# Delta-rule recurrence: the products of the inverses with the right-hand side in four quarters of the array, batch 1's chunks exchanged over the partitions

## The chip, the core and the metric

The kernel runs on one core of a Trainium2 chip. TensorE (PE in the profile, its weight loads PEld) multiplies, VectorE (DVE), ScalarE (ACT) and GpSimd (POOL) do the elementwise work, and POOL and SyncE (SP) issue most of the transfers. The metric is the device time of one execution in microseconds (us).

## What is computed

One encoder layer on two batches of 256 tokens, float32. The part that the change touches is the gated delta rule of 8 heads, run in both directions over 4 chunks of 64 tokens. Per head and direction the reference does this, where `u` and `w` are products of the inverse `t_mat` of a 64 by 64 triangular matrix:

```python
def step(S, inp):
    q_i, k_i, u_i, w_i, g_i, qk_i = inp
    v_new = u_i - einsum('bhcd,bhde->bhce', w_i, S)
    o = einsum('bhcd,bhde->bhce', q_i * exp(g_i), S) + einsum('bhcs,bhse->bhce', qk_i, v_new)
    S = S * exp(g_last) + einsum('bhcd,bhce->bhde', k_i * exp(g_last - g_i), v_new)
    return S, o
```

## The kernel before

Nearly all of the time is matrix products: `half_gemm` multiplies 8 weight blocks of 128 by 128, each split into a high and a low part, with 512 token columns; these are the rows `ps_g`. The recurrence is threaded between them. `recur` is a generator, one for each head, and two heads (h and h+1) run side by side (`recur_pair`, `together`): what one head issues up to its next `yield` is followed directly by what the other issues. `half_gemm` calls `pump` after every second weight block, and each call lets the generators go on by one `yield`; `pause(n)` skips n calls. TensorE's instructions keep exactly the order in which they are written (`pin`), so TensorE stands still when one of them has to wait. ACT's and DVE's order is set by a scheduler; `load_w` asks it to put the split of a weight block (`w_hi` on ACT, `w_lo` on DVE) ahead of other work.

Each head has 4 steps (`st`). A partition half (`half[hf]`) carries one chunk of one direction, and a step treats both halves of both batches b. In a step:

- `pks` (from step 1 on): four products of the keys and queries with the state S.
- `rv`: the right-hand side, four DVE operations, from `pks`. In step 0 it is a slice of `dvn`, so the products of step 0 are named `dvn,uq` in the profile and those of steps 1 to 3 `r,uq`.
- `os`: four ACT operations (DVE in step 2) that also read `pks`.
- `pn`: the product of the inverse in `uq[st]` with `rv`, 128 by 128 per batch. Half of the 128 by 128 matrix is zero: it holds a 64 by 64 block in two opposite corners, and `open_recurrence` clears the tiles once for that.
- `n`: an ACT copy of `pn` out of PSUM, both batches in one operation of 128 by 256 elements.
- after `pause(N_GAP)`: the new state from `n` and `kd` (rows `n,kd`), and the output part from `n` and `uq` (rows `ps_o<-n,uq`), four products each.

PSUM tiles for all of these come from the pool `psm`, which has three buffers (`sm_tile`). A fourth tile can be written only when the last reader of an earlier one is done. The tiles of the state come half from `psm`, half from the pool `pg`, and the output accumulates in two banks of their own, `O[0]` and `O[1]`.

`prepare` transposes and scales the keys into `kd`. `fetch_step` loads the inverses of one step of the head that comes two later, by POOL.

Of the kernel before, what the change touches and what calls it, by code (L numbers as in the profile page):

```python
# [8 lines left out]
F32 = mybir.dt.float32  # L9
# [14 lines left out]
NB = 2  # L24
# [50 lines left out]
def hybrid_encoder(ctx: ExitStack, tc: tile.TileContext, xT, w_in, w_ba, w_out, w_gate,  # L75
# [10 lines left out]
    def mm(*a, **k):  # L86
        pin(nc.tensor.matmul(*a, **k))  # L87
# [159 lines left out]
    def sm_tile():  # L247
        return psm.tile([P, T], F32, tag="s", name="ps_s")
# [514 lines left out]
    def open_recurrence():  # L763
        if state or vector_work:
            return
        ln_cm.__exit__(None, None, None)
        dr = dr_cm.__enter__()
        UQ = []
        for i in range(2):
            UQ.append([dr.tile([P, NB, 2, P], F32, tag=f"uq{i}{t}", name=f"uq{i}") for t in range(4)])  # L770
            for u in UQ[i]:
                nc.gpsimd.memset(u, 0.0)
        state.update(dr=dr, UQ=UQ,
                     dmix=cp.tile([P, 2, H, T], F32R, tag="c", name="dmix"))

    prepared, outputs, gate, traced, finished = {}, {}, {}, set(), set()

    fetched = {}
    def fetch(h):
# [5 lines left out]
    def fetch_step(h, t):  # L785

        u = state["UQ"][h % 2][t]
        for w in range(2):
            for hf in range(2):
                at = (1 - hf, hf)[w]  # L790
                pin(nc.gpsimd.dma_start(
                    u[half[(hf, 1 - hf)[w]], :, w, at * C:at * C + C],
                    s_uq[LN[hf, t] // 16, h * NB:h * NB + NB, :, w].rearrange("b s c -> s b c")))

    def prepare(h, vT):

        dr = state["dr"]
        while h > 1 and not {h - 2, h - 2 ^ 1} <= traced:
            yield
        if h not in fetched:  # L800
            fetch(h)
        uq, kq = fetched[h]
        yield from pause(3 + h % 2)
        pv, pk = sm_tile(), sm_tile()
        for i in range(4):
            transpose(pv[:, i * P:i * P + P], vT[:, i * P:i * P + P], ident)
        for i in range(4):
            transpose(pk[:, i * P:i * P + P], kq[:, i, 1:3].rearrange("p w c -> p (w c)"), ident)
        vn = na.tile([P, NB, 2, P], F32, tag=("vT", "s1")[h % 2], name="dvn")
        nc.scalar.copy(vn, pv.rearrange("p (b q d) -> p b q d", b=NB, q=2))  # L810
        kd = dr.tile([P, 3, NB, P], F32, tag="kd", bufs=2, name="kd")
        pk4 = pk.rearrange("p (b q d) -> p b q d", b=NB, q=2)
        for st in range(3):
            pp = 0 if st in (0, 3) else 1
            tt(kd[:, st], pk4[:, :, pp],
               scs[:, st, h * NB:h * NB + NB, None].broadcast_to([P, NB, P]), ALU.mult)
        prepared[h] = (uq, kq, vn, kd)
        yield

    def recur(h, O):  # L820
# [4 lines left out]
        for st in range(4):  # L825
            pp = 0 if st in (0, 3) else 1

            dirs = (0, 1) if st < 2 else (1, 0)
            later = []
            if S is None:  # L830
                rv = vn[:, :, pp]
            else:
                yield from pause(S_GAP)

                pks = sm_tile().rearrange("p (f b e) -> p f b e", f=2, b=NB)
                for hf in range(2):
                    for b in range(NB):
                        two = kq[:, 2 * b + pp, 2 - 2 * hf:4 - 2 * hf]
                        mm(pks[:, hf, b], two.rearrange("p w c -> p (w c)"), S[:, dirs[hf], b],
                           start=True, stop=True)  # L840
                l0 = h * NB
                rv = dr.tile([P, NB, P], F32, tag=f"r{h % 2}", name="r")
                for b in range(NB):
                    for hf in range(2):
                        a = half[hf]
                        stt(rv[a, b], pks[a, hf, b], egk[a, st, l0 + b:l0 + b + 1], vn[a, b, pp],  # L846
                            ALU.mult, ALU.add)
                for hf in range(2):
                    for b in range(NB):
                        eq = egq[half[b], LN[hf, st] // 16, h:h + 1]  # L850
                        o, q = os_[half[b], pp, hf], pks[half[1 - hf], hf, b]
                        if st == 2:
                            later.append((o, q, eq, o, ALU.mult, ALU.add))
                        else:
                            act(out=o, in_=q, func=AF.Copy, scale=eq)  # L855
                yield from pause(R_GAP)
            pn = sm_tile()
            pn3 = pn.rearrange("p (w b e) -> p w b e", w=2, b=NB)[:, 0]
            for b in range(NB):
                mm(pn3[:, b], uq[st][:, b, 0], rv[:, b], start=True, stop=True)  # L860
            n = dr.tile([P, NB, P], F32, tag=f"n{h % 2}", name="n")
            nc.scalar.copy(n, pn3)
            for a in later:
                stt(*a)
            yield from pause(N_GAP)
            if st < 3:
                pS = [None, None]
                for hf in range(2):
                    t = sm_tile() if hf else pg.tile([P, T], F32, tag="g", name="ps_s")
                    pS[dirs[hf]] = t[:, :2 * P].rearrange("p (b e) -> p b e", b=NB)  # L870
                for b in range(NB):
                    for hf in range(2):
                        a = half[1 - hf]
                        mm(pS[dirs[hf]][:, b], kd[a, st, b], n[a, b], start=True, stop=True)
                Sn = dr.tile([P, 2, NB, P], F32, tag=f"S{h % 2}", bufs=2, name="S")
                if S is None:
                    for d in range(2):
                        nc.scalar.copy(Sn[:, d], pS[d])
                else:
                    for d in range(2):  # L880
                        ch = st if d == 0 else 3 - st
                        for b in range(NB):
                            lane = d * 64 + ch * 16 + h * NB + b
                            stt(Sn[:, d, b], S[:, d, b], egl[:, lane:lane + 1], pS[d][:, b],
                                ALU.mult, ALU.add)
                S = Sn
                yield LEVEL
            for b in range(NB):
                for hf in range(2):
                    a = half[1 - hf]  # L890
                    mm(O[hf][half[b], h % 2, pp], uq[st][a, b, 1, hf * C:hf * C + C],
                       n[a, b], start=(st == 0 and h % 2 == 0), stop=(st > 1),
                       skip_group_check=True)
            if h + 2 < H:
                fetch_step(h + 2, st)
        traced.add(h)
# [727 lines left out]
```

## Time and profile before

| | us |
|---|---|
| median of 3 runs | 2236.98 |
| lowest and highest | 2236.86, 2237.53 |
| the profiled execution | 2237.35 |
| its span, first to last instruction | 2235.5 |
| TensorE busy | 2225.0 |
| VectorE, ScalarE, GpSimd busy | 1801.5, 1042.4, 318.6 |

The granted clock of TensorE is at its upper level, 2.4 GHz, in every slice. The profiled execution lies 0.37 us above the median of the runs. The recurrence stands between 520 and 780 us. How to read the rows further down: a timeline row gives the start, how long it lasts and the engine, and "x8" merges neighbouring instructions of one kind. An fp32 product shows as two matmul records with a weight load each, so the 2 + 2 products of `pn` for two heads are eight records. Matmuls are pipelined, so a row's length is longer than what it costs; the distance from start to start is the cost.

### The profile page before, as it was taken

To read this page: it belongs to the slowest core of one execution; us is meant where nothing else is said; L and a number is where in the kernel's file an instruction comes from. 1 tells how busy PE (TensorE), PEld (TensorE's weight loads), DVE (VectorE), ACT (ScalarE), POOL (GpSimd) and SP (SyncE) were. 2 spreads that over 40 slices of the span, in tenths; PEclk is the share of its full clock that TensorE was granted. 3 is DMA by queue.
4 is the path that set the end of the run, shared out by engine and by line. 5 is a ranking of instruction groups with operands and counts; after the bars stand their busy time and mean duration, and the time that the engine had idled before them with its cause. 6 is when DMAs were issued, how large, how long until landed. Compare 5 with 4: busy or idle time off the path is not lost.

```text
span 2235.5 us, 32623 instructions
## 1 busy us (share of the span) xinstructions
PE 2225.0 (100%) x12292; PEld 1911.5 (86%) x12292; DVE 1801.5 (81%) x2741; ACT 1042.4 (47%) x1545; POOL 318.6 (14%) x504
## 2 busy tenths in 40 slices
PE   9999999999999999999999999999999999999998
PEld 7888888888888888888888888888888888888888
DVE  7954799975676747898888888888888788889886
ACT  6554434333444426644444444444444464454446
POOL 1532000023322011111001111101100110011100
PEclk9999999999999999999999999999999999999999
DMA  5445433253333555778777787877777487668872
GB/s 204 140 139 151 122 110 101 102 155 100 102 103 124 180 182 185 211 201 218 202 210 204 200 213 194 221 204 209 199 194 195 140 249 198 182 204 219 222 209 86
DMA packets 115326, 390.27 MB, mean 175 GB/s; under 512 B 16064, under 2 KB 16784, under 8 KB 114400
## 3 DMA queue, kind: packets, MB, share of 16 engines
q1 hardware_dynamic: 76256, 266.37, 35.6%
q0 software_dynamic: 37328, 118.91, 25.1%
q10 hardware_dynamic: 1584, 2.89, 0.4%
q8 instruction: 97, 1.59, 0.3%
q14 instruction: 61, 0.50, 0.1%
HBM read 350.61 MB, written 37.51 MB: 174 GB/s over the span
## 4 chain that ended last, share of the span: by engine, by line
PE 98%; DVE 1%; ACT 1%; DMA 1%; issue 0%; SPq 0%; ACTq 0%
PE ps_g L87 38%; PE ps_c L87 15%; PE ps_d L87 15%; PE ps_a L87 15%; PE ps_b L87 7%; PE ps_s L87 6%; PE ps_s L90 1%; PE ps_e L87 1%; PE ps_o L87 0%; DMA x_raw<-in_xT_dram 0%; DMA nml<-s_na 0%; DVE r L846 0%; PE ps_ba L87 0%; DVE cacc L380 0%; ACT os L855 0%
## 5 line engine op out<-in xcount | busy, mean ns | idle before, releaser
L87 PE MATMUL ps_g<-xhi,w_hi 128*128 128x512 f32 x880 | 352.5, 401 | 0.6 <-ACT xhi L264 0.6
L87 PE MATMUL ps_g<-xhi,w_lo 128*128 128x512 f32 x880 | 343.6, 390 | 0.0
L87 PE MATMUL ps_g<-xlo,w_hi 128*128 128x512 f32 x880 | 340.3, 390 | 0.0
L146 ACT ACTIVATE w_hi<-b 128x1024 fp32r<-128x1024 f32 x180 | 191.0, 1061 | 231.2 <-issue 116.3
L146 ACT ACTIVATE w_hi<-w_raw 128x1024 fp32r<-128x1024 f32 x158 | 167.1, 1057 | 258.4 <-PE ps_g L87 232.5
L146 ACT ACTIVATE w_hi<-w_first 128x1024 fp32r<-128x1024 f32 x180 | 190.6, 1059 | 206.6 <-PE ps_c L87 92.0
L147 DVE TENSOR_TENSOR w_lo<-w_raw,w_hi 128x1024 fp32r<-128x1024 f32 x158 | 193.0, 1221 | 94.5 <-ACT w_hi L146 94.1
L147 DVE TENSOR_TENSOR w_lo<-w_first,w_hi 128x1024 fp32r<-128x1024 f32 x180 | 220.1, 1223 | 59.0 <-ACT w_hi L146 57.4
L147 DVE TENSOR_TENSOR w_lo<-b,w_hi 128x1024 fp32r<-128x1024 f32 x180 | 219.6, 1220 | 6.9 <-ACT w_hi L146 6.3
L87 PEld LDWEIGHTS ps_g<-xhi,w_hi 128*128 128x128 f32 x880 | 165.3, 188 | 39.3 <-issue 4.9
L87 PEld LDWEIGHTS ps_g<-xhi,w_lo 128*128 128x128 f32 x880 | 165.2, 188 | 35.8 <-DVE w_lo L283 0.2
L87 PEld LDWEIGHTS ps_g<-xlo,w_hi 128*128 128x128 f32 x880 | 165.3, 188 | 32.6 <-DVE xlo L265 0.5
L87 PE MATMUL ps_d<-xc,w_hi 128*128 128x512 f32 x704 | 175.1, 391 | 0.0
L87 PE MATMUL ps_c<-xc,w_hi 128*128 128x512 f32 x704 | 175.1, 391 | 0.0
L87 PE MATMUL ps_a<-xc,w_hi 128*128 128x512 f32 x696 | 173.1, 391 | 0.0
L87 PEld LDWEIGHTS ps_c<-xc,w_hi 128*128 128x128 f32 x704 | 129.4, 188 | 25.0
L87 PEld LDWEIGHTS ps_d<-xc,w_hi 128*128 128x128 f32 x704 | 129.3, 188 | 25.0
L87 PEld LDWEIGHTS ps_a<-xc,w_hi 128*128 128x128 f32 x696 | 127.9, 188 | 24.8
L146 ACT ACTIVATE w_hi<-w_second 128x1024 fp32r<-128x1024 f32 x60 | 63.7, 1061 | 103.1 <-PE ps_d L87 67.5
L87 PE MATMUL ps_d<-xc,w_lo 128*128 128x256 f32 x704 | 98.5, 283 | 0.0
L87 PE MATMUL ps_c<-xc,w_lo 128*128 128x256 f32 x704 | 98.5, 283 | 0.0
L87 PE MATMUL ps_a<-xc,w_lo 128*128 128x256 f32 x696 | 97.4, 283 | 0.0
(420 smaller groups left out, 4319.0 us busy)
## 6 DMA issues: line engine op xcount, KB each, us to landing
w_raw<-in_w_in_dram SPq DMA_DIRECT2D x108, 512.0 KB, 3.4
b<-in_w_gate_dram SPq DMA_DIRECT2D x66, 512.0 KB, 3.8
b<-in_w_up_dram SPq DMA_DIRECT2D x66, 512.0 KB, 4.0
b<-in_w_group_dram SPq DMA_DIRECT2D x48, 512.0 KB, 4.4
w_raw<-in_w_out_dram SPq DMA_DIRECT2D x32, 512.0 KB, 3.6
raw_q<-s_act POOLq DMA_DIRECT2D x24, 512.0 KB, 5.1
w_second<-in_w_gate_dram SPq DMA_DIRECT2D x22, 512.0 KB, 7.0
w_first<-in_w_gate_dram SPq DMA_DIRECT2D x22, 512.0 KB, 5.5
```

What stands on the lines that cost most here:

```text
L87: pin(nc.tensor.matmul(*a, **k))
L90: pin(nc.tensor.transpose(*a))
L146: act(out=hi, in_=src, func=AF.Copy)
L147: tt(lo, src, r32(hi), ALU.subtract)
```

## The change

The two 64 by 64 blocks of each inverse are now stored without the zeros (`uq` has a width of 64 instead of 128), and `pn` is four products of 64 rows by 64 columns, each in its own quarter of the array. So that the four quarters differ, batch 1's chunks are kept in the same partition half, while batch 0's are exchanged as before; `place` says where a chunk's result goes. `n`, `kd`, the state's products and the output's products follow the new places. Batch 0's product goes to a new `psm` tile, batch 1's to a second new one in step 0 and, from step 1 on, to the first 128 columns of the `pks` tile, which has been read by then; `n` is copied per batch. In step 2 the first of the four `os` operations is issued ahead of the product, since it reads that place.

```diff
-            UQ.append([dr.tile([P, NB, 2, P], F32, tag=f"uq{i}{t}", name=f"uq{i}") for t in range(4)])
-            for u in UQ[i]:
-                nc.gpsimd.memset(u, 0.0)
+            UQ.append([dr.tile([P, NB, 2, C], F32, tag=f"uq{i}{t}", name=f"uq{i}") for t in range(4)])
...
+    def place(hf, b):
+
+        return half[hf if b else 1 - hf]
+
+    QUADS = ((0, 0), (0, 1), (1, 1), (1, 0))
...
-        for w in range(2):
-            for hf in range(2):
-                at = (1 - hf, hf)[w]
-                pin(nc.gpsimd.dma_start(
-                    u[half[(hf, 1 - hf)[w]], :, w, at * C:at * C + C],
-                    s_uq[LN[hf, t] // 16, h * NB:h * NB + NB, :, w].rearrange("b s c -> s b c")))
+        n = h * NB
+        for hf in range(2):
+            src = s_uq[LN[hf, t] // 16, n:n + NB].rearrange("b s w c -> w s b c")
+            pin(nc.gpsimd.dma_start(u[half[hf], :, 0], src[0]))
+        for hf in range(2):
+            src = s_uq[LN[hf, t] // 16, n:n + NB].rearrange("b s w c -> w s b c")
+            for b in range(NB):
+                pin(nc.gpsimd.dma_start(u[place(hf, b), b, 1], src[1, :, b]))
...
-            tt(kd[:, st], pk4[:, :, pp],
-               scs[:, st, h * NB:h * NB + NB, None].broadcast_to([P, NB, P]), ALU.mult)
+            for b, to, a in ((0, slice(0, P), slice(0, P)), (1, *half), (1, *half[::-1])):
+                n = h * NB + b
+                f = scs[a, st, n:n + 1]
+                tt(kd[to, st, b], pk4[a, b, pp], f.broadcast_to(list(kd[to, st, b].shape)), ALU.mult)
...
-            pn = sm_tile()
-            pn3 = pn.rearrange("p (w b e) -> p w b e", w=2, b=NB)[:, 0]
+            pn = [sm_tile()[:, :P], pks[:, 0, 0] if st else sm_tile()[:, :P]]
+            for b, hf in QUADS:
+                mm(pn[b][place(hf, b)], uq[st][half[hf], b, 0], rv[half[hf], b],
+                   start=True, stop=True)
+            n = dr.tile([P, NB, P], F32, tag=f"n{h % 2}", name="n")
             for b in range(NB):
-                mm(pn3[:, b], uq[st][:, b, 0], rv[:, b], start=True, stop=True)
-            n = dr.tile([P, NB, P], F32, tag=f"n{h % 2}", name="n")
-            nc.scalar.copy(n, pn3)
+                nc.scalar.copy(n[:, b], pn[b])
...
-            for b in range(NB):
-                for hf in range(2):
-                    a = half[1 - hf]
-                    mm(O[hf][half[b], h % 2, pp], uq[st][a, b, 1, hf * C:hf * C + C],
-                       n[a, b], start=(st == 0 and h % 2 == 0), stop=(st > 1),
-                       skip_group_check=True)
+            for b, hf in QUADS:
+                a = place(hf, b)
+                mm(O[hf][half[b], h % 2, pp], uq[st][a, b, 1], n[a, b],
+                   start=(st == 0 and h % 2 == 0), stop=(st > 1), skip_group_check=True)
```

TensorE's order stays as it was but for `pn` itself. In step 1 of the first two heads (`uq_4349` and `uq_4357` before, `uq_4353` now, are the inverses of the two heads; `ps_g` rows are the large product around it; the names in brackets are the counters that an instruction waits for, `Activation` being ACT's, `DMASW` a POOL transfer's) TensorE's rows were before:

```order
L87 MATMUL ps_g<-xhi_109,w_lo 128x512
L87 MATMUL ps_s<-r,uq_4349 128x128 [waits DMASW6_49,DMASW7_49,DVE_49,PE_49]
L87 MATMUL ps_s<-r,uq_4349 128x128 [waits DVE_49]
L87 MATMUL ps_s<-r,uq_4357 128x128 [waits DVE_49,DMASW2_49,PE_49,DMASW3_49,Activation_49,Pool_49]
L87 MATMUL ps_s<-r,uq_4357 128x128 [waits DVE_49]
L87 MATMUL ps_g<-xhi_108,w_hi 128x512
```

and are now:

```order
L87 MATMUL ps_g<-xhi_109,w_lo 128x512
L87 MATMUL ps_s<-r,uq_4349 64x128 [waits DMASW2_49,DVE_49]
L87 MATMUL ps_s<-r,uq_4349 64x128 [waits DMASW3_49,DVE_49]
L87 MATMUL ps_s<-r,uq_4349 64x128 [waits DVE_49,Activation_49]
L87 MATMUL ps_s<-r,uq_4349 64x128
L87 MATMUL ps_s<-r,uq_4353 64x128 [waits DMASW0_49,DVE_49,Activation_49]
L87 MATMUL ps_s<-r,uq_4353 64x128 [waits DMASW1_49,DVE_49]
L87 MATMUL ps_s<-r,uq_4353 64x128 [waits DVE_49]
L87 MATMUL ps_s<-r,uq_4353 64x128
L87 MATMUL ps_g<-xhi_108,w_hi 128x512
```

Nothing moved past anything else; two products per head became four, and head h+1's first still carries a wait for ACT.

On ACT, around the copies of `n` in steps 0 and 1 of the first two heads (`dvn` is the right-hand side of step 0, `ev_vn` and `ev_s` are gates that get their SiLU), the order was before:

```order
L810 COPY dvn<-ps_s 128x512 x2
L146 ACTIVATE w_hi<-w_raw 128x1024
L862 COPY n<-ps_s 128x256 x2
L991 ACTIVATE ev_vn<-ev_vn 128x512
L878 COPY S<-ps_s 128x256 x4
L146 ACTIVATE w_hi<-w_raw 128x1024
L855 ACTIVATE os<-ps_s,egq 64x128 x8
L146 ACTIVATE w_hi<-w_raw 128x1024
L862 COPY n<-ps_s 128x256 x2
```

and is now:

```order
L816 COPY dvn<-ps_s 128x512 x2
L146 ACTIVATE w_hi<-w_raw 128x1024
L873 COPY n<-ps_s 128x128 x3
L1000 ACTIVATE ev_vn<-ev_vn 128x512
L873 COPY n<-ps_s 128x128
L888 COPY S<-ps_s 128x2x128
L889 COPY S<-ps_s 128x256
L888 COPY S<-ps_s 128x2x128
L889 COPY S<-ps_s 128x256
L146 ACTIVATE w_hi<-w_raw 128x1024
L865 ACTIVATE os<-ps_s,egq 64x128 x8
L146 ACTIVATE w_hi<-w_raw 128x1024
```

Two copies of `n` per step became four smaller ones, behind the same weight split. In step 1 of the third pair of heads the SiLU stood between the two copies of `n`:

```order
L149 ACTIVATE dmix<-yo,dnw 128x512 x2
L146 ACTIVATE w_hi<-w_raw 128x1024
L855 ACTIVATE os<-ps_s,egq 64x128 x8
L862 COPY n<-ps_s 128x256
L991 ACTIVATE ev_s_6038<-ev_s_6038 128x512
L862 COPY n<-ps_s 128x256
```

and now stands ahead of all four:

```order
L149 ACTIVATE dmix<-yo,dnw 128x512 x2
L146 ACTIVATE w_hi<-w_raw 128x1024
L865 ACTIVATE os<-ps_s,egq 64x128 x8
L1000 ACTIVATE ev_s_6178<-ev_s_6178 128x512
L873 COPY n<-ps_s 128x128 x4
```

There the gate's SiLU has moved ahead of the first copy.

## Rows read from the trace of the kernel before

**Rows 1.** The page: the chain that ended last, by engine.
```profile
PE 98%; DVE 1%; ACT 1%; DMA 1%; issue 0%; SPq 0%; ACTq 0%
```
**Rows 2.** Groups by form, PE: shapes, count, busy us, mean ns, idle before.
```profile
L87 PE MATMUL ps_s<-r,uq 128*128 128x128 f32 x96 | 13.1, 276 | 0.8 <-ACT n L862 0.5 <-PE ps_s L87 0.3
...
L87 PE MATMUL ps_o<-n,uq 64*64 64x128 f32 x256 | 10.7, 282 | 0.0
```
**Rows 3.** Timeline, PE, 574.6 to 580.0: start, length, instruction, count.
```profile
574.88 0.39 PE L87 MATMUL ps_g<-xhi,w_lo 128*128 128x512 f32 x1
575.11 1.05 PE L87 MATMUL ps_s<-r,uq 128*128 128x128 f32 x8
...
576.23 0.39 PE L87 MATMUL ps_g<-xlo,w_hi 128*128 128x512 f32 x1
...
578.52 0.39 PE L87 MATMUL ps_g<-xhi,w_lo 128*128 128x512 f32 x1
578.84 0.67 PE L87 MATMUL ps_o<-n,uq 64*64 64x128 f32 x16
579.44 0.50 PE L87 MATMUL ps_g<-xhi,w_hi 128*128 128x512 f32 x1
579.78 0.40 PE L87 MATMUL ps_g<-xlo,w_hi 128*128 128x512 f32 x1
```
**Rows 4.** Timeline, all engines, 526 to 534: step 0 of the first two heads.
```profile
528.38 1.06 ACT L146 ACTIVATE w_hi<-w_raw 128x1024 fp32r<-128x1024 f32 x1 [3.68 <-PE ps_g L87]
528.40 1.05 PE L87 MATMUL ps_s<-dvn,uq 128*128 128x128 f32 x8
...
529.34 0.63 ACT L862 COPY n<-ps_s 128x256 f32<-128x256 f32 x2
...
532.14 1.16 PE L87 MATMUL ps_s<-n,kd 64*128 64x128 f32 x16
...
533.24 0.67 PE L87 MATMUL ps_o<-n,uq 64*64 64x128 f32 x16
```
**Rows 5.** Timeline, all engines, 686.0 to 688.6: step 2 of the third pair.
```profile
686.09 0.39 PE L87 MATMUL ps_g<-xhi,w_lo 128*128 128x512 f32 x1
...
686.32 0.61 PE L87 MATMUL ps_s<-r,uq 128*128 128x128 f32 x4
...
687.00 0.35 DVE L864 SCALAR_TENSOR_TENSOR os<-ps_s,egq,os 64x128 f32<-64x128 f32 x1
687.02 0.37 ACT L862 COPY n<-ps_s 128x256 f32<-128x256 f32 x1 [1.08 <-PE ps_s L87]
...
687.44 0.71 PE L87 MATMUL ps_s<-r,uq 128*128 128x128 f32 x4 [0.52 <-ACT n L862]
...
688.23 0.40 PE L87 MATMUL ps_g<-xlo,w_hi 128*128 128x512 f32 x1
```
**Rows 6.** Timeline, all engines, 752.0 to 754.2: step 2 of the fourth pair.
```profile
752.21 0.39 PE L87 MATMUL ps_g<-nmh,w_lo 128*128 128x512 f32 x1
...
754.05 0.40 PE L87 MATMUL ps_g<-nml,w_hi 128*128 128x512 f32 x1
```
**Rows 7.** Timeline, all engines, 735.0 to 738.9: step 1 of the fourth pair.
```profile
735.60 1.05 PE L87 MATMUL ps_s<-r,uq 128*128 128x128 f32 x8
...
738.19 0.63 ACT L862 COPY n<-ps_s 128x256 f32<-128x256 f32 x2
738.56 0.50 PE L87 MATMUL ps_g<-nml,w_hi 128*128 128x512 f32 x1 [0.98 <-DVE nml L147]
```
**Rows 8.** Groups by form, ACT: a gate's SiLU, and a copy from PSUM.
```profile
L991 ACT ACTIVATE ev_s<-ev_s 128x512 f32<-128x512 f32 x2 | 1.3, 638 | 0.0
...
L568 ACT COPY egl<-ps_s 128x128 f32<-128x128 f32 x1 | 0.2, 247 | 0.0
```
**Rows 9.** Groups by form: DVE's scaling of the keys, POOL's loads of the inverses.
```profile
L815 DVE TENSOR_TENSOR kd<-ps_s,tab 128x256 f32<-128x256 f32 x24 | 8.8, 417 | 3.0 <-PE ps_s L90 3.0
...
L791 POOL DMA_DIRECT2D uq<-s_uq x128 | 74.6, 599 | 149.1 <-PE ps_s L87 101.3 <-PE ps_o L87 40.6 <-DMA s_uq<-kkq 5.8
```

More of the change, by code (lines that the diff above doesn't have):

```diff
@@ L851, in recur @@
                         o, q = os_[half[b], pp, hf], pks[half[1 - hf], hf, b]
-                        if st == 2:
+                        if st == 2 and hf + b:
                             later.append((o, q, eq, o, ALU.mult, ALU.add))
+                        elif st == 2:
+                            stt(o, q, eq, o, ALU.mult, ALU.add)
                         else:
@@ L866, in recur @@
             if st < 3:
-                pS = [None, None]
-                for hf in range(2):
-                    t = sm_tile() if hf else pg.tile([P, T], F32, tag="g", name="ps_s")
-                    pS[dirs[hf]] = t[:, :2 * P].rearrange("p (b e) -> p b e", b=NB)
-                for b in range(NB):
-                    for hf in range(2):
-                        a = half[1 - hf]
-                        mm(pS[dirs[hf]][:, b], kd[a, st, b], n[a, b], start=True, stop=True)
+                two = [t[:, :2 * P].rearrange("p (i e) -> p i e", i=2)
+                       for t in (pg.tile([P, T], F32, tag="g", name="ps_s"), sm_tile())]
+                pS = {}
+                for b, hf in QUADS:
+                    r = hf if b else 1 - hf
+                    pS[dirs[hf], b] = two[r][:, b if r else 1 - b]
+                    mm(pS[dirs[hf], b], kd[half[r], st, b], n[half[r], b], start=True, stop=True)
                 Sn = dr.tile([P, 2, NB, P], F32, tag=f"S{h % 2}", bufs=2, name="S")
                 if S is None:
-                    for d in range(2):
-                        nc.scalar.copy(Sn[:, d], pS[d])
+                    Sf = Sn.rearrange("p d b e -> p (d b) e")
+                    nc.scalar.copy(Sf[:, 0::3], two[1])
+                    nc.scalar.copy(Sf[:, 1:3], two[0])
                 else:
@@ L883, in recur @@
                             lane = d * 64 + ch * 16 + h * NB + b
-                            stt(Sn[:, d, b], S[:, d, b], egl[:, lane:lane + 1], pS[d][:, b],
+                            stt(Sn[:, d, b], S[:, d, b], egl[:, lane:lane + 1], pS[d, b],
                                 ALU.mult, ALU.add)
@@ L887, in recur @@
                 yield LEVEL
-            for b in range(NB):
-                for hf in range(2):
-                    a = half[1 - hf]
-                    mm(O[hf][half[b], h % 2, pp], uq[st][a, b, 1, hf * C:hf * C + C],
-                       n[a, b], start=(st == 0 and h % 2 == 0), stop=(st > 1),
-                       skip_group_check=True)
+            for b, hf in QUADS:
+                a = place(hf, b)
+                mm(O[hf][half[b], h % 2, pp], uq[st][a, b, 1], n[a, b],
+                   start=(st == 0 and h % 2 == 0), stop=(st > 1), skip_group_check=True)
             if h + 2 < H:
```

## The prediction, made before the changed kernel ran

> **What bounds the kernel now.** I read the page first. The chain that ended last lies on TensorE for 98% [rows 1], so each microsecond for which TensorE is held up, or that it is spared, comes back in the span, and work on the other engines counts only where TensorE waits for it. The reader should then look at the recurrence between 520 and 780 us, where the change lies: in the timeline the products `pn` of two heads stand as one block of eight records between `ps_g` rows. There are 16 such blocks, one for each of four steps and four pairs of heads. From the last `ps_g` start ahead of a block to the second `ps_g` start behind it, a block without a wait takes 576.23 - 574.88 = 1.35 us [rows 3]; two `ps_g` alone would take 0.45 of that. Last I looked at what a block waits for: 14 of the 16 wait for nothing, two do, and these two decide how I read the change.
>
> **Why those two wait.** `psm` has three buffers. In steps 1 to 3 the two `pks` tiles and head h's `pn` fill them, so the `pn` of head h+1 goes into the buffer of head h's `pks` and must wait until that has been read. In step 2 of the third pair a DVE `os` from 687.00 to 687.35 was late, and TensorE's second half started at 687.44 and not at 686.32 + 0.45 = 686.77; the block took 688.23 - 686.09 = 2.14 us, 0.79 too long [rows 5]. In step 2 of the fourth pair it took 754.05 - 752.21 = 1.84, 0.49 too long [rows 6]. So a buffer that comes free late stops TensorE, and 1.28 us of that is in the time before.
>
> **Part 1, the product itself.** Two full products per head become four quarters. The nearest rows are the output's products, which already are 64 by 64 in the four quarters: 16 records of two heads, alone between `ps_g` rows, take 579.78 - 578.52 = 1.26 us [rows 3]. The new block has the same number of records in the same four quarters, so it should cost 1.26 instead of 1.35, a gain of 0.09, 1.4 us in 16 blocks. This is far less than the count of columns suggests, because the array changes its mode at both ends: the first quarter starts 0.32 after the last `ps_g`, where a full product starts 0.23 after it [rows 3].
>
> **Part 2, the new wait.** This is the term that decides. From step 1 on head h keeps its `pks` buffer for batch 1's product, and so does head h+1; only the third buffer is left, and both heads' batch 0 products need it. In step 0 the two heads want four buffers of three. So in all 16 blocks a product of head h+1 stands behind ACT's copy of head h's batch 0, which itself cannot start before head h's first two quarters are done. In the old program the copy was needed only later, by `n,kd`, which starts 532.14 - 529.97 = 2.17 us after the copies in step 0 have ended [rows 4]. Behind the waiting product on TensorE stands the whole `ps_g` stream, that is, everything.
>
> The price, with T the start of the old block. If ACT is idle: the new block starts 0.09 later (0.32 against 0.23). The 16 records of the output start within 0.67 - 0.28 = 0.39 (length in rows 3, mean of one in rows 2), four at a time in four waves; I put 0.16 for the first, whose weight load lies in the open, and 0.11 for each further. The second wave then starts at +0.16 and lasts 0.27: the first two quarters are done at T + 0.52. ACT starts a copy 0.09 after the last record that it waits for (686.32 + 0.61 = 686.93, copy at 687.02) [rows 5], so at A = T + 0.61. A copy of 128 by 128 out of PSUM took 0.25 [rows 8]; the old one of 128 by 256 took 0.37 [rows 5]. I take 0.25, the row of the same shape, and 0.37 for the upper end. From the end of a releaser to TensorE's restart it is 0.09 (687.35 to 687.44) [rows 5]. TensorE starts again at R = A + 0.34. From a first quarter to the second `ps_g` a block of 16 took 579.78 - 578.84 = 0.94 [rows 3]; with 8 records two waves of 0.11 are missing, so 0.72. The old block ended at T + 1.12 (576.23 - 575.11). The loss is therefore R + 0.72 - T - 1.12 = (A - T) - 0.06, with the gain of part 1 in it. With ACT idle that is 0.55.
>
> ACT is often not idle. In step 0 of the first pair a weight split of 1.06 us starts with the block, and the copy comes at 529.34, A - T = 0.94 [rows 4]; the split stands ahead of the copies in the new order too, so the loss is 0.88. I took A - T from the sixteen copies in this way (16 rows: the first stands in rows 4, the fourteenth, which is the latest of all against its block, in rows 7), except where ACT was waiting for TensorE, where A is the idle value. The 16 losses in order of time: 0.88, 0.93, 0.92, 0.87 (first pair); 0.55, 1.20, 0.90, 1.30 (second); 0.55, 1.82, 0.55, 1.43 (third); 0.99, 2.53, 0.55, 0.81 (fourth). Two were moved by hand: in step 1 of the third pair the gate's SiLU of 0.64 [rows 8] is now ahead of the copies, and in step 0 of the fourth pair DVE's longer `kd` (part 3) delays a SiLU that stands ahead. The 2.53 is 738.19 - 735.60 = 2.59 less 0.06 [rows 7]: there ACT copies last, behind four `os` and a SiLU. The sum is 16.8 us.
>
> Against it go the two old waits, 1.28 us: the `pks` buffer that caused them is no longer what head h+1's first quarter needs. And the 0.98 us for which TensorE waits for DVE at 738.56, after the largest of the stalls, is swallowed by it [rows 7]. Sum of part 2 with part 1: 16.8 - 1.3 - 1.0 = +14.5 us.
>
> **Part 3, the rest, which I cost at nothing.** `kd` becomes 9 DVE operations per head instead of 3. An operation of 256 elements took 0.417 in the mean and three of them 8.8/8 = 1.1 us of DVE per head [rows 9]; at half the elements I estimate 1.8 to 2.2 us, 0.7 to 1.1 more per head, 6 to 9 us of DVE in all. It is hidden by the pauses between a head's transposes and its first product (two calls of `pump`, six `ps_g` of 0.23 each, are 2.7 us), except for the one SiLU counted above; if that cover were gone it would be at most those 9 us. POOL issues 192 loads of the inverses instead of 128, at 0.6 each [rows 9], 38 us more; POOL waited 149 us of that stretch for TensorE, and a load is used a whole pair of heads later. What is queued behind them on POOL, the stores of `h`, is wanted only after the recurrence. The clears that go were POOL's, too. The extra ACT copies (four of 0.25 instead of two of 0.37) cost ACT 0.3 us a block, ahead of `n,kd`, which has 2.17 us to spare [rows 4]. `n,kd` keeps one bank for each partition half and its order. That leaves the banks of `pn` and of the output's products. Before, the products from partitions 0 to 63 wrote `O[1]` and those from 64 to 127 `O[0]`, so that a bank took results from one half of the array's rows; now each bank, of `O` as of `pn`, takes one result from each half, into different partitions. No row shows that case. I take no cost, since each partition still gets results of a bank from one quarter only; the upper end is the next rival.
>
> **The Trainium skill** has a rule here, in "TensorEngine Tiling (Array Packing)", section "Restrictions and Gotchas": different row tiles cannot access the same PSUM bank simultaneously. By it the quarters would go two by two and the time would be that of the second rival; the trace before neither shows nor excludes it.
>
> **The rivals.** (1) *The wait is paid at its idle price everywhere*, because TensorE's own standstills give ACT time to catch up: 16 x 0.55 - 1.28 = +7.5, 2244.5 (this and the times that follow stand on the median's scale). For it: the late copies are late against a TensorE that never stopped. Against it: the splits and the `os` in front of the copies are themselves released by TensorE's products, so they move with it. I count it as the low edge of my forecast. (2) *Quarters that share a bank take turns.* The nearest row of two at a time is `n,kd`: 16 records from 532.14 to 533.24, 1.10 us, against 0.60 for the output's 16 (0.94 less the 0.34 to the second `ps_g`) [rows 3, 4]. That adds 0.50 x 16 = 8.0 on the output and 0.22 a half block on `pn`, where it also delays the copy: 0.22 x 21 = 4.6, as 5 blocks have an idle ACT. With the forecast: +27.1, 2264.1. (3) *Not slower: the copies come in time and the change does what it says.* This ends on the other side. It decides from the point where the buffer of head h's batch 0 is free before head h+1 wants it, that is, where ACT's copy ends within 0.2 us of the quarters. Price: 1.4 + 1.3 = 2.7 us gained, 2234.3. Against it: 0.52 + 0.09 + 0.25 us cannot be hidden, as nothing stands between the two heads' products. (4) *The count of records decides*: 128 full records at 13.1/96 = 0.136 us become 256 at 10.7/256 = 0.042 [rows 2], 17.4 - 10.7 = 6.7 us gained and the two waits too, 2229.0. Against it: the ends of the blocks, shown in part 1.
>
> **How the numbers follow.** The sum is made against the profiled execution: 2237.35 + 14.5 = 2251.9. That execution lies 0.37 above the median of the runs, so I forecast 2251.5, on the median's scale. Chances: the forecast with its low edge 0.78, bank turns 0.14, gain as in (3) 0.05, (4) 0.01, something slower still 0.02. The range reaches from rival (1) with a shorter handover, 2243, to rival (2), 2264; with the copy at 0.37 the forecast itself would be 2253.4. A measurement of this kernel can tell some 0.2%, 4.5 us, from no change. Rival (3) lies within it, rival (4) and part of a gain that I don't see beyond it: faster 0.02, same 0.05, slower 0.93.
>
> **What would show it.** In the changed profile: eight records of a block as 4 + 4 in groups with a gap of 0.5 to 2.5 us between the two heads' products, released by ACT's copy of `n`, 16 times, some 10 to 14 us of TensorE's idle time in all. A block's quarters should start four at a time, and the output's 16 records should still take 0.60; if they take 1.10, rival (2) holds. The two waits for DVE in step 2 should be gone, and so should the 0.98 for `nml`. If TensorE shows no gap between the heads, the reading of the buffers is wrong; if the gaps are all near 0.6, rival (1) is right. The time between 784 us and the end should not change.

## The result, and the profile after

The changed kernel is slower: 2256.25 us median of five runs (2253.85 to 2258.36) against 2236.98 before. The ratio is 1.0085, with a 95% interval from 1.0073 to 1.0096, that is +19.3 us. The profiled execution took 2257.72, with a span of 2255.8 us against 2235.5. All of the difference arises in the recurrence: from the first `pn` product (528.40 before, 528.67 after) to the last `ident,os` (784.62 and 805.31) it is 20.4 us longer, and from there to TensorE's last product it is 1444.0 us in both.

What TensorE waits for, by the view of the waits (engine, line, what it waited for: us in total, times, longest):

```profile
PE ps_s L87 <- ACT n L873: 13.1, 15, 2.7
...
PE ps_s L90 <- DVE os L939: 0.9, 1, 0.9
PE ps_s L87 <- DVE yo L956: 0.8, 1, 0.8
```

The first line is the wait that the prediction speaks of; the other two were not in it. The wait for `nml` [rows 7] is gone. One block whole, from the timeline of all engines, with ACT free when the quarters end (start, length, instruction, count, and in brackets the idle time with its releaser; it answers to rows 3):

```profile
630.33 0.39 PE L87 MATMUL ps_g<-xhi,w_lo 128*128 128x512 f32 x1
...
630.65 0.45 PE L87 MATMUL ps_s<-r,uq 64*64 64x128 f32 x8
631.22 0.43 ACT L873 COPY n<-ps_s 128x128 f32<-128x128 f32 x2 [0.27 <-PE ps_s L87]
...
631.53 0.55 PE L87 MATMUL ps_s<-r,uq 64*64 64x128 f32 x8 [0.43 <-ACT n L873]
...
632.35 0.40 PE L87 MATMUL ps_g<-xlo,w_hi 128*128 128x512 f32 x1
```

The first `ps_s` row is the eight records of head h's quarters; then comes a hole of 0.43 us in which ACT copies, and then the eight of head h+1. The block takes 632.35 - 630.33 = 2.02 us, where it took 1.35 [rows 3]. So it is in the twelve blocks of steps 1 to 3. In step 0 the hole lies further back, behind twelve records and ahead of the last four, since there the third buffer takes head h+1's first product and only its second has to wait, as here in the third pair:

```profile
664.88 0.43 PE L87 MATMUL ps_s<-dvn,uq 64*64 64x128 f32 x4 [0.17 <-ACT n L873]
```

The longest block is the one that answers to rows 7:

```profile
751.30 0.73 ACT L865 ACTIVATE os<-ps_s,egq 64x128 f32<-64x128 f32 x2
...
751.86 0.66 PE L87 MATMUL ps_s<-r,uq 64*64 64x128 f32 x8
...
752.84 1.49 ACT L865 ACTIVATE os<-ps_s,egq 64x128 f32<-64x128 f32 x4 [0.81 <-DVE r L854]
...
754.35 0.63 ACT L1000 ACTIVATE ev_zs<-ev_zs 128x512 f32<-128x512 f32 x1
...
754.89 0.41 ACT L873 COPY n<-ps_s 128x128 f32<-128x128 f32 x2
...
755.19 0.58 PE L87 MATMUL ps_s<-r,uq 64*64 64x128 f32 x8 [2.67 <-ACT n L873]
```

Ahead of the copies ACT has `os` of both heads and the gate's SiLU, and of the `os` four are themselves held up for DVE's `r` until 752.84. TensorE stands for 2.67 us.

Over the 16 blocks, taken as in the prediction from the last `ps_g` start ahead to the second behind, less 1.35 each:

| pair | predicted, steps 0 to 3 | measured |
|---|---|---|
| 1 | 0.88, 0.93, 0.92, 0.87 | 0.81, 0.98, 0.98, 1.36 |
| 2 | 0.55, 1.20, 0.90, 1.30 | 0.50, 1.26, 0.67, 1.35 |
| 3 | 0.55, 1.82, 0.55, 1.43 | 0.50, 1.92, 0.66, 1.49 |
| 4 | 0.99, 2.53, 0.55, 0.81 | 0.72, 3.40, 0.66, 0.94 |
| sum | 16.8 | 18.2 |

The view of stretches shows one thing more (stretch; length; busy time of PE, PEld, DVE, ACT, POOL with counts; granted clock; DMA):

```profile
670.00:680.00 10.00, 10.00 (x56) 8.64 (x57) 5.86 (x15) 3.48 (x6) 5.32 (x10) 1.00 0.24 74
680.00:690.00 10.00, 8.36 (x66) 5.94 (x66) 3.12 (x8) 4.63 (x13) 1.21 (x3) 0.83 0.17 59
...
750.00:762.00 12.00, 9.33 (x70) 6.80 (x69) 7.98 (x17) 5.42 (x15) 0.00 (x0) 0.86 0.77 296
```

Where TensorE has just stood in the two longest waits (blocks at 681.04 and 751.86), the granted clock falls from 2.4 to 1.2 GHz: the mean of 0.83 over ten microseconds is some 3.4 us at the lower level, each time. From 683.99 to 684.42 `ps_g` products start 0.43 us apart instead of 0.23. Thirteen such intervals together are 2.6 us too long. Of the five runs the two shortest were granted the whole clock, the two longest 0.998.

### The profile page after: what moved, and what is told of

It is laid out like the page before. It is cut to its first block, busy times and chain, and to the rows that moved or that the text cites. A ratio compares the mean times of both kernels' runs of the same rounds, so it can differ in the third digit from the quotient of the medians.

```text
span 2255.8 us, 33015 instructions
## 1 busy us (share of the span) xinstructions
PE 2232.1 (99%) x12420; PEld 1906.8 (85%) x12420; DVE 1814.2 (80%) x2789; ACT 1045.3 (46%) x1577; POOL 343.7 (15%) x560
## 4 chain that ended last, share of the span: by engine, by line
PE 95%; ACT 2%; DVE 2%; DMA 1%; issue 1%; SPq 0%; ACTq 0%; DVEq 0%
PE ps_g L87 36%; PE ps_c L87 15%; PE ps_d L87 15%; PE ps_a L87 14%; PE ps_b L87 7%; PE ps_s L87 6%; ACT os L865 1%; PE ps_s L90 1%; DVE kd L824 1%; PE ps_e L87 1%; DVE r L854 0%; PE ps_o L87 0%; ACT w_hi L146 0%; DMA x_raw<-in_xT_dram 0%; DMA nml<-s_na 0%
```

## The experiments

The theory: the second head's quarters wait for ACT's copy of the first head's, and that is the loss. The rivals: the quarters themselves, the exchange with its loads, or the count of buffers. The ratios are against runs of the kernel before that were taken together with each run, on the same chip (medians 2237.25 for the first four, 2237.56 for the next four, 2237.38 for the last). The column of blocks is the sum taken as above; it was 1.3 before.

| run | median us | ratio, 95% interval | 16 blocks |
|---|---|---|---|
| e1_one_tile | 2256.53 | 1.0087 [1.0073, 1.0101] | 18.5 |
| e2_both_before_copies | 2242.97 | 1.0027 [1.0016, 1.0037] | 3.0 |
| e3_wait_alone | 2255.45 | 1.0080 [1.0066, 1.0094] | 19.7 |
| e4_exchange_alone | 2242.92 | 1.0024 [1.0015, 1.0034] | 1.9 |
| e5_short_kd | 2237.75 | 1.0000 [0.9991, 1.0009] | 2.0 |
| e6_both_short_kd | 2237.84 | 1.0004 [0.9995, 1.0013] | 2.7 |
| e7_both_short_kd_os_late | 2236.72 | 0.9996 [0.9987, 1.0005] | -0.4 |
| e8_os_late | 2252.37 | 1.0066 [1.0054, 1.0079] | 13.6 |
| e9_after_short_kd | 2252.79 | 1.0071 [1.0058, 1.0085] | 18.1 |

### e1: fewer buffers, the same order

```diff
-            pn = [sm_tile()[:, :P], pks[:, 0, 0] if st else sm_tile()[:, :P]]
+            i = h % 2
+            if not i:
+                state["pn"] = [sm_tile() for _ in range(1 if st else 2)]
+            own = [t[:, i * P:i * P + P] for t in state["pn"]]
+            pn = [own[0], pks[:, 0, 0] if st else own[1]]
```

> The changed kernel with one edit: the products of the inverses of both heads stand side by side in one PSUM tile, so that the second head needs no third buffer of its own. The order of all instructions stays: first the four quarters of head h, then ACT's copy of them, then the four quarters of head h+1. Theory (the products of head h+1 wait for ACT's copy of head h, whichever way they are tied to it): the second head's first quarter now writes into the very bank that the copy reads, so the wait stays, and the 16 blocks lose 15 to 19 us against the kernel before; 2253 to 2258 us. Rival (only the count of three buffers makes the wait): it goes with the third tile, and the time is 2234 to 2239 us.

```profile
PE ps_s L87 <- ACT n L877: 14.4, 16, 2.7
```

2256.53, as in the changed kernel. The prediction tied the wait to three buffers of `psm`. That is how it comes about there, but doing without the third buffer is no cure: a product into a tile that ACT is still reading waits just as long, though it writes other columns. The profile infers its releasers from the counters that a program sets, so this wait, too, stands in the program; whether the chip would need it no run shows. A fourth buffer was not tried.

### e2: the same tile, both heads ahead of both copies

```diff
                    start=True, stop=True)
+            yield LEVEL
             n = dr.tile([P, NB, P], F32, tag=f"n{h % 2}", name="n")
```

> As the run with one tile, and one line more: each head hands over once its four quarters are written down, so that the quarters of both heads stand ahead of both heads' copies. No instruction is added or taken away. Theory (the wait for the copy is the whole loss): TensorE meets no copy of n within the 16 blocks. From the kernel before: -1.4 us for the quarters, -1.3 us and -1.0 us for the two kinds of old waits that the shift swallows, -0.6 us for an old wait ahead of ident,kq, and +2.6 us for three late DVE results (os 1.4, yo 1.0, kd 0.2) that the longer kd causes: 2235.3 us, 2233 to 2238; the granted clock is whole throughout the recurrence. Rival (the quarters themselves are slow where two of them share a bank, or the extra loads and DVE operations cost the time): 2248 to 2256 us, the blocks long without any wait for ACT.

The line makes each head hand over to the other when its quarters are written down. It only moves instructions, and it takes 13.6 us off e1. A block now, from the timeline of PE:

```profile
527.91 0.39 PE L87 MATMUL ps_g<-xhi,w_lo 128*128 128x512 f32 x1
528.23 0.67 PE L87 MATMUL ps_s<-dvn,uq 64*64 64x128 f32 x16
528.82 0.50 PE L87 MATMUL ps_g<-xhi,w_hi 128*128 128x512 f32 x1
529.16 0.40 PE L87 MATMUL ps_g<-xlo,w_hi 128*128 128x512 f32 x1
```

529.16 - 527.91 = 1.25 us: all sixteen quarters in one go, 0.10 below the 1.35 of before, in 12 of the 16 blocks. So part 1 of the prediction (1.26, a gain of 0.09) is right. But the time is 5 us above the upper end of what I expected (2238), so something else costs too. Its waits:

```profile
PE ps_s L87 <- ACT os L865: 2.5, 3, 1.7
PE ps_s L90 <- DVE os L944: 1.9, 1, 1.9
PE ps_s L87 <- DVE yo L961: 1.5, 1, 1.5
```

The waits for DVE's `os` and `yo` are larger than in the changed kernel, and batch 1's quarters, which write into the tile of `pks`, now wait for ACT's reading of it.

### e3: the wait alone

```diff
-            pn = sm_tile()
+            if h % 2 == 0:
+                state["pn"] = sm_tile()
+            pn = state["pn"]
```

> The kernel before with one edit: both heads' products of the inverses, still whole 128x128 ones, go to one PSUM tile, the second head's beside the first's, in the order of before. So the second head's products wait for ACT's copy of the first head's, as in the changed kernel, but there are no quarters, no exchange, no further loads and DVE operations. Theory: 16 waits of 0.6 to 3 us as in the changed kernel, 16 to 19 us in sum, and up to 3.4 us more if the clock falls to its lower level behind the longest two: 2252 to 2259 us. Rival (quarters, exchange or loads make the loss): 2237 to 2240 us.

This is the kernel before, whole products, no exchange, and it takes 2255.45. By itself the wait gives +18.2 us, so it needs neither quarters nor exchange. The trace has it 16 times, four of them without a releaser that the profile could name:

```profile
PE ps_s L87 <- ACT n L864: 11.7, 12, 2.9
PE ps_s L87 <- issue: 3.2, 4, 0.8
```

### e4: the exchange alone

The changed kernel with these lines in place of its quarters (and with the inverses' tiles of the kernel before, cleared and filled in eight loads per step):

```diff
-            pn = [sm_tile()[:, :P], pks[:, 0, 0] if st else sm_tile()[:, :P]]
-            for b, hf in QUADS:
-                mm(pn[b][place(hf, b)], uq[st][half[hf], b, 0], rv[half[hf], b],
-                   start=True, stop=True)
+            pn = sm_tile()
+            pn3 = pn.rearrange("p (w b e) -> p w b e", w=2, b=NB)[:, 0]
...
+                mm(pn3[:, b], uq[st][:, b, 0], rv[:, b], start=True, stop=True)
```

> The changed kernel with its exchange over the partitions, its nine kd operations per head, its further loads on POOL and its order of the O products, but with whole 128x128 products of the inverses and one copy of both batches, as in the kernel before. Theory: no wait for a copy of n beyond the old ones of 1.3 us; the longer kd costs 1.4 us at os and 1.0 us at yo, the 0.65 us ahead of ident,kq go: 2237 to 2240 us. Rival (the exchange, its loads or the banks are what costs): 2248 us or more.

2242.92: my expectation missed again, by 2.9 us from its upper end. There is no wait for a copy of `n` here beyond the old one, yet 5.7 us are lost. The timeline of DVE and PE where the second pair's keys are scaled shows where:

```profile
585.25 5.45 DVE L827 TENSOR_TENSOR kd<-ps_s,tab 128x128 f32<-128x128 f32 x18
590.73 0.17 DVE L935 TENSOR_SCALAR ssq<-ssq 128x8 f32<-128x8 f32 x1
...
594.41 1.43 DVE L941 TENSOR_TENSOR os<-os,ssq 128x256 f32<-128x256 f32 x4
```

```profile
592.86 0.40 PE L87 MATMUL ps_g<-xhi,w_lo 128*128 128x512 f32 x1
595.32 1.38 PE L90 MATMUL ps_s<-ident,os 128*128 128x128 f32 x8 [2.06 <-DVE os L941]
596.37 0.76 PE L87 MATMUL ps_g<-xhi,w_hi 128*128 128x512 f32 x1
596.92 0.63 PE L87 MATMUL ps_g<-xlo,w_hi 128*128 128x512 f32 x1
```

In the kernel before the same place reads:

```profile
585.34 1.08 DVE L815 TENSOR_TENSOR kd<-ps_s,tab 128x256 f32<-128x256 f32 x3
...
587.81 1.08 DVE L815 TENSOR_TENSOR kd<-ps_s,tab 128x256 f32<-128x256 f32 x3
```

Twice 1.08 us of `kd` have become 5.45. Behind it on DVE stand the norm of the pair before and its `os`, and TensorE, which wants to transpose that `os`, stands for 2.06 us. After that the next `ps_g` rows start 0.43 us apart: the clock has fallen, and it does so again behind the wait for `yo` (the view of stretches has 0.83 in 590 to 600 and in 730 to 740).

### e5: the exchange with a short kd

```diff
+        kx = state["dr"].tile([P, 2, 2, C], F32, tag="kx", bufs=2, name="kx")
+        for w in range(2):
+            nc.sync.dma_start(kx[:, :, w], s_kq[h, :, 2:4, 2 - w])
...
-            transpose(pk[:, i * P:i * P + P], kq[:, i, 1:3].rearrange("p w c -> p (w c)"), ident)
+            two = kq[:, i, 1:3] if i < 2 else kx[:, i - 2]
+            transpose(pk[:, i * P:i * P + P], two.rearrange("p w c -> p (w c)"), ident)
...
-            for b, to, a in ((0, slice(0, P), slice(0, P)), (1, *half), (1, *half[::-1])):
...
+            tt(kd[:, st], pk4[:, :, pp],
+               scs[:, st, h * NB:h * NB + NB, None].broadcast_to([P, NB, P]), ALU.mult)
```

> The run with the exchange alone took 2242.9 us where 2237 to 2240 was expected; in its trace DVE works on 18 kd operations from 585.3 to 590.7 us, where the kernel before needs 1.1 us for each of two heads, and TensorE waits 2.1 us for os and 1.9 us for yo later on. This run is that kernel with kd alone put back to three operations per head: batch 1's key chunks are loaded a second time in exchanged order, so that the transposes already deliver them in their new partitions, and the small table of factors is exchanged once. Products, POOL's loads, order and output stay (and the inverses' tile is packed tighter to make room). Theory (the longer kd on DVE is what the exchange costs): the waits for os and yo go, and what is left against the kernel before is -0.65 to +1 us: 2236 to 2239 us. Rival (POOL's loads, the exchanged partitions or the O order cost it): it stays at 2241 to 2244 us.

2237.75, the time of before. The waits for `os` and `yo` are gone, and those that are left are old ones, this among them:

```profile
PE ps_g L87 <- DVE nml L147: 1.0, 1, 1.0
```

So the longer `kd` is all that the exchange costs, 5.2 us by the two medians. The 64 further loads on POOL (here 128, as the loads are split once more), the exchanged partitions and the new order of the output's products cost nothing that this measurement can tell.

### e6 and e7: without either cost

e6 is e2 with the short `kd` of e5.

> The run with the quarters of both heads ahead of the copies (2243.0 us) with the same short kd: three operations per head from key chunks loaded in exchanged order. Theory: of its losses, the waits for os (1.9 us) and yo (1.5 us) and what the lower clock costs behind them go; the waits of batch 1's quarters for ACT's os (2.5 us and more), which write into the bank that those still read, stay: 2236 to 2240 us. Rival (the quarters cost something of their own): 2242 us or more.

e7 also sets three of the four `os` of a head behind the copies of `n` (`do` is the operation, kept as a function, on ACT in steps 1 and 3 and on DVE in step 2):

```diff
-                        if st == 2 and hf + b:
-                            later.append((o, q, eq, o, ALU.mult, ALU.add))
...
+                        if hf + b:
+                            later.append(do)
+                        else:
+                            do()
```

> As the run before it, and of the four os operations per head only the one that reads the columns which batch 1's quarters overwrite stays ahead of the products; the other three come behind the copies of n. Theory: batch 1's quarters wait for one os instead of four, so most of the 4.5 us that these waits add in steps 2 and 3 go, and with the shorter blocks (0.10 us each, 1.6 us in all) the time ends below that of the kernel before: 2232 to 2236 us. Rival (an os set back makes the products behind it late, or os comes too late for the end of the pair): 2238 us or more.

e6 takes 2237.84 and e7 2236.72, 19.5 us less than the changed kernel, with all of its quarters and its exchange. Against the kernel before, neither can be told from no change. The block that e2 showed has the same 0.67 us for sixteen quarters in both; in e7, 15 of the 16 blocks gain their 0.10, as expected. The time below 2236 that I expected of e7 did not come. Its waits say where the gain went:

```profile
PE ps_s L87 <- DVE yo L967: 0.9, 1, 0.9
PE ps_s L87 <- ACT os L867: 0.8, 1, 0.8
PE ps_s L87 <- DVE ev_xi L325: 0.8, 1, 0.8
```

The last one, at 563 us, stands in e2 and e6 as well. Taken as excess over the same places of before, these three are 1.2, 1.1 and 1.2 us, and three smaller ones, at 586, 627 and 783 us, are 0.4, 0.2 and 0.6. Against them stand the 1.5 that the quarters gain and some 3 us of old waits that are gone or shorter (1.3 in the blocks, 1.3 at `nml`, 0.3 ahead of `ident,kq`). The two sides about cancel: what TensorE saves in one place it waits for in another.

### e8: the price of the wait

> The changed kernel with that last edit alone: three of four os operations per head behind the copies of n. The wait of head h+1's quarters for the copies stays, but ACT has less ahead of them in those blocks where os stood there (five of the sixteen, the two longest among them). Theory (the price of a block is what ACT has ahead of the copy): some 4.5 us of the waits go, and the clock's fall behind the two longest with them, up to 3.4 us; the blocks with a weight split or a SiLU ahead stay as they are: 2247 to 2253 us. Rival (the price is set by the wait itself, or the work ahead only trades places): 2254 to 2258 us.

The edit of e7 alone, in the changed kernel. The 16 blocks fall from 18.2 to 13.6 us, 4.6 less, where I had expected 4.5; 11 of them now cost 0.50 to 0.67, the price with ACT free. The time falls by 3.9, to 2252.37, or by 4.5 when each kernel is taken against its own runs of before (+19.3 and +14.8); with a spread of 4.5 and 3.2 us between their runs the two cannot be told apart. The clock's fall did not go: it still falls twice, once behind the longest block and once behind the wait for `os`, which has grown from 0.9 to 1.9. That leaves the time at the upper end of what was expected.

```profile
PE ps_s L87 <- ACT n L875: 8.3, 14, 2.2
PE ps_s L90 <- DVE os L941: 1.9, 1, 1.9
```

### e9: the long kd beside the wait

> The changed kernel with the short kd alone (three operations per head, from key chunks loaded in exchanged order); the wait of head h+1's quarters for ACT's copy stays. With the runs before it this fills a square: kd long or short, the wait there or not. Without the wait the long kd cost 2243.0 - 2237.8 = 5.1 us. Theory (the two costs overlap: while TensorE stands at the 16 waits, DVE catches up): with the wait the long kd costs only what the changed kernel's trace shows of it, 1.4 us at os, 1.1 at yo and 0.2 at n,kd, so this run takes 2252 to 2254.5 us. Rival (the costs add up): 2256.3 - 5.1 = 2251 us or less. Rival (the long kd costs nothing beside the wait, as it was costed): 2255.5 to 2257 us.

2252.79. In its trace the waits for `os` and `yo` are gone and the blocks cost 18.1, as in the changed kernel. The square:

| | kd long | kd short |
|---|---|---|
| wait for the copy there | 2256.25 | 2252.79 |
| wait gone | 2242.97 | 2237.84 |

By these medians the long `kd` costs 3.5 us beside the wait and 5.1 without it; each against its own runs of before, it is 3.9 and 5.4. The intervals in the upper row overlap (1.0073 to 1.0096 and 1.0058 to 1.0085), and a difference of 1.5 between the two prices is within the noise: the times alone do not rule out that the costs add up. The traces speak for the overlap. TensorE waits 0.9 us for `os` and 0.8 for `yo` in the changed kernel and 1.9 and 1.5 in e2, where it stands less before. The profiled executions of the changed kernel and of e9 are 5.2 us apart, but 2.6 of that is the clock, which did not fall in e9's; 2.6 are left. The 0.2 at `n,kd`, which I had put down to the long `kd`, stands in e9 as well.

## Why the prediction was right, and where it was not

**The deciding term held.** Forecast +14.5 us and 2251.5, measured +19.3 and 2256.25, within the range. All 16 blocks have the hole, in steps 1 to 3 between the two heads and in step 0 within head h+1; the view of the waits names ACT's copy of `n` in 15 and lists none for the first block. 13.1 us of idle time were inside the 10 to 14 named. A block has sixteen records and not the eight that the prediction's last paragraph counts, so they stand as 8 + 8 or 12 + 4. Most blocks come near the price worked out from the old copies, with 18.2 instead of 16.8 in sum; e3 shows that the wait alone makes a loss of this size, and e8 that what ACT has ahead of a copy sets its price. The largest miss but one is step 3 of the first pair, 1.36 instead of 0.87: there the eight `os`, late by a wait for DVE's `r`, ended 0.3 us behind the block's start and pushed the weight split ahead of the copy. The two old waits of 1.28 and the 0.98 for `nml` are gone, as said. Outside the recurrence nothing changed. That the time stayed in the range is in part luck: two terms of some 2.5 us each, the longer `kd` and the clock, were in no sum, and the range was wide enough for them only because its upper end was the price of rival (2), which is out.

**The idle price was 0.66, not 0.55, from step 1 on.** The step that failed is the end of the block, put at 0.72 from a first quarter to the second `ps_g`; in the rows above it is 632.35 - 631.53 = 0.82. I took off two waves of 0.11 as if the four quarters behind the hole started together; they do not. The first goes alone, at 631.53, and the other three follow from 631.64; so it is in each of the twelve blocks. The timeline of PE cut to 631.5 to 631.6 has one record where the row above merges eight:

```profile
631.53 0.32 PE L87 MATMUL ps_s<-r,uq 64*64 64x128 f32 x1 [0.43 <-ACT n L873]
```

Why it goes alone was not tried. In step 0, where only four records stand behind the hole, the measured price is 0.50.

**The block of 2.53 measured 3.40.** I moved the old copy's time over unchanged: 2.59 us behind the block's start [rows 7]. It came at 754.89 - 751.86 = 3.03, since the last four `os` ahead of it had to wait for DVE's `r` until 752.84 (the row above with 0.81 idle), and DVE in turn was late from the `yo` of the pair before. The longer `kd` is not the reason: in e9, without it, the block has the same wait of 2.67. The rest of the 0.87 is the first quarter's later start and the end of the block, 756.29 - 755.19 = 1.10, with the clock already falling.

**Part 3, costed at nothing, was wrong.** Two steps failed. The size: I estimated 1.8 to 2.2 us for a head's nine operations. They take (13.8 + 7.0) / 8 = 2.6, so 12.0 us more in all and not 6 to 9, as the groups by form show of the changed kernel:

```profile
L824 DVE TENSOR_TENSOR kd<-ps_s,tab 64x128 f32<-64x128 f32 x48 | 13.8, 288 | 0.7
...
L824 DVE TENSOR_TENSOR kd<-ps_s,tab 128x128 f32<-128x128 f32 x24 | 7.0, 292 | 3.4 <-PE ps_s L90 3.0
```

Against 0.417 us for 128x256 [rows 9], half the elements save 0.125 of it, and half the partitions nothing. And the cover: I asked who waits for `kd`, which is `n,kd` and far off, and not who stands behind it on DVE. That is the norm of the pair before, for which TensorE waits. In the changed kernel this is 1.4 us at `os` and 1.1 at `yo`, counted from start to start; e5 and e9 show it as 5.2 without the wait and about 3.5 beside it. Of POOL, the same part read the 149 us of idle time as spent on TensorE; it is 101.3 + 40.6 = 141.9 [rows 9], and nothing hung on it.

The Trainium skill bears on this in "Perfetto Trace Analysis", section "Optimizing Scalar/DVE Operations": each operation of VectorE carries an access overhead of its own, larger for a PSUM operand, and grouping into larger operations can help if the engine is saturated. The trace agrees with the overhead: the mean went from 417 to 288 and 292 ns, and the count from 24 to 72. But DVE was not saturated here, busy for 172.66 of the 257 us from 528 to 785 before and for 170.63 of them after, two thirds, and the smaller operations cost time all the same.

**The clock was in no term.** It is 2.6 us of the profiled execution.

Together, on the profiled executions, from start to start: 18.2 - 1.3 = +16.9 for the blocks, +2.6 for `os`, `yo` and `n,kd`, -1.3 for `nml` (the wait of 0.98 and the slower restart behind it), -0.6 for a wait ahead of `ident,kq` that went, +2.6 for the clock: 20.2, where the recurrence is 20.4 longer.

**The rivals.** Rival (1), the idle price everywhere, is out: 11 blocks cost more. Rival (2), quarters that share a bank take turns, is out: the output's sixteen records still take 0.67 as a row, as in rows 4, although each bank now takes results from both halves of the rows:

```profile
534.22 0.67 PE L87 MATMUL ps_o<-n,uq 64*64 64x128 f32 x16
```

Rival (3) named the right point, where the copy comes in time, but no copy can; e2 gets there by order instead. Rival (4) stays out: a block without a wait gains 0.10, not what the count of records says.

**Left open.** A fourth buffer of `psm` was not tried, so the wait was lifted by order alone. That the gain of the quarters in e6 and e7 is given back in later waits was seen in their traces, and not tried apart. Quarters of both batches into one bank were not tried, since two of them would write the same partitions of that bank at the same time.

## What to carry to other kernels

A product that is split to be cheaper needs a place for its parts; count the buffers, and see in which order products and copies are written down, since two products ahead of two copies did not stop the engine at the copy, where product, copy, product, copy did. An operation that grows on an engine with time to spare still delays what is queued behind it there, so ask who waits for that, and not only who waits for the operation itself. Two costs that are both waits of one engine need not add up, and removing the larger one can bring out more of the other: the wait for `os` grew from 0.9 to 1.9 us when the wait for the copy went.

## What the runs showed of the hardware

Quarters from both halves of the array's rows went into one PSUM bank at the same pace as quarters from one half, as long as they wrote different partitions: 0.67 us for the sixteen records of the output, four starting within 0.02 us, two for each of the two banks. Before the change, when a bank took results from one half alone, it was 0.67 as well. The Trainium skill has a wider rule in "TensorEngine Tiling (Array Packing)", section "Restrictions and Gotchas", by which different row tiles cannot access one bank at the same time; by it these records would have needed the time of rival (2). The measurement decides: here it did not hold for different partitions.

TensorE's granted clock fell to 1.2 GHz behind single waits in the middle of dense work. In the profiled executions this was behind waits of 1.64 and 2.67 us in the changed kernel (blocks at 681.04 and 751.86), of 1.64 in e1, 2.88 in e3, 2.06 and 1.91 in e4, and 1.91 and 2.19 in e8. Each time the view of stretches has 0.83 over ten microseconds, some 3.4 us at 1.2 GHz, and 1.00 in the next. It did not fall behind the shorter waits of the changed kernel, nor behind any wait of e2 and e9, with 1.9 and 2.7 us among them, nor in e1 behind the same block's 2.7. So a wait of this length may cost the clock and may not, and the runs of one kernel differ by it: the five of the changed kernel, from 2253.85 to 2258.36, have mean clocks of 1.000, 1.000, 0.999, 0.998 and 0.998 in this order. They spread over 4.5 us, the 27 runs of the kernel before that were taken with e5 to e8 over 2.4.
